# A query/key tile holds 32 channels of four heads in place of 64 channels of two, and one norm sum and root serve two tiles

## The chip, the cores and the metric

The kernel runs on one core of a Trainium2 chip. The metric is the time of one execution on the device in microseconds (us); the kernel is run several times and the median is shown. The core's engines have a queue of instructions each and run beside one another: TensorE (PE, matrix products, with a second queue PEld for loading weights), VectorE (DVE), ScalarE (ACT), GpSimd (POOL) and SyncE (SP, which here only starts transfers). An engine takes its instructions in order, so one that waits holds up everything behind it on that engine. Transfers run on 16 DMA engines.

## The reference

One layer of a hybrid encoder block on 1024 tokens of 1024 channels. After an RMS norm, one projection `z = h @ w_in` yields queries, keys and values for three attention groups of eight heads (64 channels each), and the gates and inputs of a gated linear recurrence. The part that the change concerns is the norm of queries and keys, for every token and every head over that head's 64 channels:

```
def rms_norm(t, w):
    t32 = t.astype(jnp.float32)
    return t32 * lax.rsqrt(jnp.mean(t32 * t32, axis=-1, keepdims=True) + EPS) * w.astype(jnp.float32)
...
for g, (window, dilation) in enumerate(ATTN_GROUPS):      # (128,1), (512,4), (2048,16)
    q = rms_norm(qkv_a[:, :, g, 0], q_norm_w[layer, g])
    k = rms_norm(qkv_a[:, :, g, 1], k_norm_w[layer, g])
    v = qkv_a[:, :, g, 2]
    o_g, m_g, d_g = dilated_window_attention(q, k, v, bias_tab[:, ...], window, dilation)
```

The attention takes scores `q . k` over the 64 channels of a head, adds a bias by distance, applies a softmax over a band of keys and sums the values. The recurrence branch, the two gates and the output projection follow and are left as they are.

## The kernel before

The program is straight-line code, written by a planner: class `Plan` keeps an estimated clock for each engine, and `Builder` emits instructions by it. Work that isn't on the main line stands in lists: `task` entries (for ACT, DVE, POOL and SP) and `product` entries (small matrix products for PE). `tick` emits a task when its inputs are due, by the plan's clocks, within `AHEAD` = 1.4 us of PE's clock; `burst` emits products between the main products. So the order on each engine is fixed when the program is built, from estimates, and the chip's waits follow from what really comes late. A `Ring` is a set of buffers of one kind, used in turn; a task can also wait for room in a ring.

The stages in order: normalising x and the value projections (to about 142 us); the **quads**, 27 blocks of the projection (142 to about 678 us); attention, mixed with projections of the recurrence's inputs (from about 685 us); the recurrence; the two output projections. The change lies in the quads and in what attention loads.

**A quad block** multiplies a 1024 x 512 piece of `w_in` with the whole input by a scheme with seven products in place of eight. Its weights come as four tiles `qraw` of 128 x 512 ("11", "12", "22", "21"), which SP loads into a ring of six (line 1098) in the order 11, 12, 22, 21 (`start_quads`, line 403). DVE subtracts tiles from one another (T1 = 12 - 11, T2 = 22 - 11 and so on); each operand is split into a high part `whi` (ACT copies it to the matmul's short float type) and a low part `wlo` (POOL, or DVE for T2 and T4, subtracts), into rings of `RING` = 9. Each of the seven products is 12 matmuls of 128 x 512 (`run_quads`, line 448). PE's order is 11(m), 22(m-1), T4(m-1), T1(m), T2(m), 21(m), T3(m), 11(m+1) and so on. Between the products ACT copies the accumulating bank `qA` after 11 and after T2, and `qE` after T1, and DVE adds the banks of 21, T3 and 22 to those copies: T2, T3 and T4 go on accumulating into `qA`, so a copy has to be out before the product after the next begins.

Twelve of the 27 blocks are query/key blocks (`qk`): group g (three), half hv of its heads (four heads each), e = 0 for queries and 1 for keys. They stand two at a time, with one or two other blocks after each two. A block's result is four tiles `z` of 128 channels x 512 tokens: col 0 or 1 (two heads of 64 channels each), half 0 or 1 of the tokens. In a `qk` block the weight tiles are read from rows of `w_in` in runs of 128 columns, so 512 bytes (`block_pages`, line 674).

**The norm** runs on each of the 48 tiles `z` by itself (lines 1124 to 1176): ACT squares z into a tile `ny` and copies it as `nhi`; DVE subtracts to get `nlo`; two matmuls with a matrix of ones, `headones` (ones in two diagonal blocks of 64 x 64), sum each head's 64 squares and spread the sum over the head's rows, in a PSUM bank `nss`; ACT takes Ln, Exp(-0.5 x) and a square; DVE ends with three operations (`newton`): a correction, z times weight (`nqk`) times root, and the two multiplied with the tokens put in the order of their residues. SP stores the tile to `qkD` in DRAM. Its rings: `ny` four, `nhi` and `nlo` two each, `spare` (z and other copies) seven.

**Attention** loads queries and keys of a (g, hv) whole, one transfer of 1 MB each, as tiles `aq` and `ak` of 128 x 2 x 1024 (`load_q` and `load_k`, lines 1253 to 1261): head 2a + i lies on the 64 partitions from 64 i, page a. Behind them come the bias `abias` and eight value tiles `av`. `scores` (line 1309) multiplies 64 partitions of `aq` and `ak` at a time into PSUM banks `sc`, and DVE adds the bias. For g = 0 one value tile is loaded as two transfers of 64 partitions (`load_v`, line 1263). The first such loads stand in SP's queue behind two transfers `stage<-h10D`.

## Time and profile before

| what | value |
|---|---|
| time, median of 3 runs (lowest, highest) | 1449.19 us (1448.72, 1449.32) |
| profiled execution: its own time, its span | 1449.3 us, 1447.5 us |
| PE busy | 1437.9 us, 99% of the span, 7930 matmuls |
| PEld busy | 1197.1 us |
| DVE, ACT, POOL busy | 967.6, 894.9, 338.8 us |
| DMA | 194992 packets, 230.75 MB; 46083 packets under 512 B |
| granted clock of PE | 1.0 |

The span runs from the first to the last instruction, and the execution's own time is 1.8 us longer. A busy share is the time in which an instruction of the engine was under way; the profile models a matmul's end, and matmuls overlap, so that the count of matmuls in a stretch says more than a matmul's own duration. "Idle before" is how long an engine waited ahead of the instruction, with the event that ended the wait. All matmul lines carry line 58, that of the recording wrapper, so rows are told apart by the tiles' names.

### The profile page before, as it was taken

The page shows a single profiled execution, that of the slowest core. Times are in us where ns is not written, and L with a number is a line of the kernel's source. Part 1 is how long each engine was busy: PE and PEld are TensorE (multiplying, and loading weights), DVE is VectorE, ACT ScalarE, POOL GpSimd, SP SyncE. Part 2 cuts the span into 40 slices and gives each one's busy share as a digit, 9 for nine tenths or more (in the row PEclk, how much of TensorE's full clock was granted, in tenths as well). Part 3 has the DMA queues.
Part 4 walks back from the last instruction along what each step waited for, and adds up shares of the span by engine and source line. Part 5 has one row for each costly group of instructions (what it writes and reads, how often), then busy time and mean ns, then how long its engine had stood idle before and what let it go on. Part 6 is the DMA issues. An engine that isn't in the chain of part 4 may idle for free.

```text
span 1447.5 us, 22946 instructions
## 1 busy us (share of the span) xinstructions
PE 1437.9 (99%) x7930; PEld 1197.1 (83%) x7930; DVE 967.6 (67%) x1901; ACT 894.9 (62%) x1900; POOL 338.8 (23%) x356
## 2 busy tenths in 40 slices
PE   9999999999999999999999999999999999999998
PEld 8788888888888888888788778888888888888887
DVE  6673677778685778331464648487878787358973
ACT  7743767566565676443688753397777774548461
POOL 0102334454423444333002000032222221001011
PEclk9999999999999999999999999999999999999999
DMA  7646567776643344324748439364444443678665
GB/s 239 181 141 197 167 195 164 196 152 167 151 124 102 102 103 115 111 103 142 267 147 292 156 101 331 120 148 103 130 106 129 107 136 87 215 243 213 189 167 137
DMA packets 194992, 230.75 MB, mean 159 GB/s; under 512 B 46083, under 2 KB 118043, under 8 KB 194364
## 3 DMA queue, kind: packets, MB, share of 16 engines
q1 hardware_dynamic: 180188, 203.93, 44.8%
q0 software_dynamic: 13824, 25.17, 11.3%
q8 instruction: 62, 1.02, 0.3%
q14 instruction: 54, 0.44, 0.1%
q10 hardware_dynamic: 864, 0.19, 0.1%
HBM read 169.29 MB, written 81.43 MB: 173 GB/s over the span
## 4 chain that ended last, share of the span: by engine, by line
PE 89%; DVE 6%; ACT 3%; issue 1%; DMA 1%; POOL 0%; SPq 0%; DVEq 0%
PE gp L58 27%; PE qA L58 20%; PE qE L58 10%; PE qC L58 5%; PE sA L58 5%; PE sE L58 4%; PE u L58 3%; PE oB L58 3%; PE o L58 3%; PE pT L58 2%; PE sc L58 2%; PE nss L58 2%; DVE Bc L58 1%; PE U L58 1%; DVE S L58 1%; DVE xs L58 1%
## 5 line engine op out<-in xcount | busy, mean ns | idle before, releaser
L58 POOL TENSOR_TENSOR wlo<-qraw,whi 128x512 fp32r<-128x512 f32 x135 | 191.7, 1425 | 380.9 <-ACT whi L58 294.4
L58 ACT ACTIVATE whi<-qraw 128x512 fp32r<-128x512 f32 x189 | 117.7, 626 | 100.6 <-DVE qraw L58 42.2
L58 DVE TENSOR_TENSOR qraw<-qraw,qraw 128x512 f32<-128x512 f32 x108 | 99.7, 924 | 36.7 <-POOL wlo L58 26.9
L58 PE MATMUL gp<-hh,whi 128*128 128x512 f32 x264 | 109.7, 416 | 0.0
L58 PE MATMUL gp<-hh,wlo 128*128 128x512 f32 x264 | 103.6, 393 | 0.0
L58 PE MATMUL gp<-hl,whi 128*128 128x512 f32 x264 | 103.0, 390 | 0.0
L58 ACT ACTIVATE as<-as,neg 128x192 f32<-128x192 f32 (+2 forms) x192 | 83.7, 440 | 18.0 <-DVE neg L58 17.9
L58 DVE CUSTOM_DVE_ANT_0 as<-sc,abias 128x192 f32<-128x192 f32 (+2 forms) x192 | 56.0, 348 | 43.7 <-PE sc L58 35.1
L58 ACT ACTIVATE whi<-raw 128x512 fp32r<-128x512 f32 x92 | 57.7, 627 | 43.9 <-PE gp L58 18.7
L58 PE MATMUL qA<-hh,whi 128*128 128x512 f32 x216 | 84.0, 389 | 0.0
L58 PE MATMUL qA<-hl,whi 128*128 128x512 f32 x216 | 84.0, 389 | 0.0
L58 PE MATMUL qA<-hh,wlo 128*128 128x512 f32 x216 | 84.0, 389 | 0.0
L58 POOL COPY mm<-Bc 128x8 f32<-128x8 f32 x64 | 32.2, 533 | 205.6 <-DVE Bc L58 123.6
L58 PE MATMUL gp<-whi,hh 128*128 128x512 f32 x192 | 78.6, 409 | 0.1
L58 PE MATMUL gp<-wlo,hh 128*128 128x512 f32 x192 | 75.2, 391 | 0.4 <-DVE wlo L58 0.4
L58 PE MATMUL gp<-whi,hl 128*128 128x512 f32 x192 | 75.0, 391 | 0.0
L58 DVE TENSOR_TENSOR wlo<-qraw,whi 128x512 fp32r<-128x512 f32 x54 | 37.3, 692 | 49.8 <-ACT whi L58 49.8
L58 DVE SCALAR_TENSOR_TENSOR ny<-ny,spare 128x512 f32<-128x512 f32 x48 | 63.2, 1316 | 1.6
L58 ACT ACTIVATE ny<-ny 128x512 f32<-128x512 f32 x96 | 60.8, 633 | 3.9 <-DVE ny L58 0.8
L58 PEld LDWEIGHTS gp<-hh,wlo 128*128 128x128 f32 x264 | 49.5, 188 | 11.0
L58 POOL DMA_DIRECT2D wlo<-in_w_in_dram x36 | 31.5, 875 | 113.6 <-ACT wlo L58 97.8
L58 ACT ACTIVATE stage<-gp 128x512 f32<-128x512 f32 x39 | 22.9, 591 | 54.9 <-PE gp L58 39.7
(306 smaller groups left out, 4232.2 us busy)
## 6 DMA issues: line engine op xcount, KB each, us to landing
qraw<-in_w_in_dram SPq DMA_DIRECT2D x108, 256.0 KB, 3.8
raw<-in_w_in_dram SPq DMA_DIRECT2D x84, 256.0 KB, 3.4
qkD<-ny SPq DMA_DIRECT2D x48, 256.0 KB, 2.8
wlo<-in_w_in_dram POOLq DMA_DIRECT2D x36, 256.0 KB, 4.1
sg<-sgD SPq DMA_DIRECT2D x32, 256.0 KB, 3.4
eraw<-wsD SPq DMA_DIRECT2D x32, 256.0 KB, 3.0
sgD<-stage SPq DMA_DIRECT2D x26, 256.0 KB, 2.6
ak<-qkD SPq DMA_DIRECT2D x6, 1024.0 KB, 6.2
```

The lines of the kernel that those rows point to most:

```text
L58: got = f(*args, **kw)
```

## The change

The channels of a `qk` block are dealt differently to its two columns: col 0 has channels 0 to 31 of all four heads, col 1 has channels 32 to 63. A row of `z` in col 0 and the same row in col 1 then belong to one head, so their squares can be added before the sum over rows, and the sum of a head (`headones` now has four blocks of 32 x 32) serves both tiles.

- The weights of a `qk` block are read in runs of 32 columns, 128 bytes, and each of the block's four tiles by four transfers, one for each head.
- `put_qk` waits until both columns of a half are there. Then ACT squares both, DVE adds the squares (`sq_sum`), ACT copies the high part (`sq_high`), DVE subtracts the low part, PE makes two matmuls, ACT takes Ln, Exp and square once; `newton` makes the correction once and the two products for each of the two columns, five operations of DVE in one go, and both are stored. A chain needs three tiles of the ring `ny` at its root, which still has four.
- The tile of norm weights has a column set for each col and is loaded by eight transfers in place of one.
- `aq` and `ak` are put together from four transfers each, of 32 partitions by 2 x 1024 (`load_heads`).

The order on each engine moves only in the quads; elsewhere on PE the rows are the same and in the same order. On PE 48 rows fall away, all of `nss`. Here PE's queue in the first `qk` blocks, names as above: before, two pairs of `nss` (of two tiles) between T2's last matmuls (`qA<-S1`) and the product 21 (`qC`),

```order
L58 MATMUL qA_1534<-S1h,wlo_1469 128x512
L58 MATMUL nss_1677<-nhi_1610,headones 128x512
L58 MATMUL nss_1677<-nlo_1641,headones 128x512
L58 MATMUL nss_1680<-nhi_1635,headones 128x512
L58 MATMUL nss_1680<-nlo_1653,headones 128x512
L58 MATMUL qC_1683<-hh_97,whi_1475 128x512
```

and of the changed kernel the only pair ahead of that product, one product earlier (`qE<-S0` is T1):

```order
L58 MATMUL qE_1639<-S0h,wlo_1476 128x512
L58 MATMUL nss_1670<-nhi_1629,headones 128x512
L58 MATMUL nss_1670<-nlo_1636,headones 128x512
L58 MATMUL qA_1562<-S1h,whi_1501 128x512
```

A pair now stands for two tiles, and there is one where there were two.

SP's queue in the quads, at the last two weight tiles of block 4, a `qk` block, and the first two of block 5, a gate (`qkD<-ny` stores a normed tile, `sgD<-stage` a gate's tile, `wsD` prepares later weights). Before:

```order
L58 DMA sgD<-stage_1836 128x512
L58 DMA wsD<-in_w_proj_b_dram 16x4096
L58 DMA qkD<-ny_1882 128x512
L58 DMA qraw_1959<-in_w_in_dram 128x4x128
L58 DMA qraw_1961<-in_w_in_dram 128x4x128
L58 DMA qraw_1967<-in_w_in_dram 128x512
L58 DMA qraw_1969<-in_w_in_dram 128x512
L58 DMA sgD<-stage_1856 128x512
```

and now:

```order
L58 DMA skewD<-tabD 128x384
L58 DMA wsD<-in_w_proj_b_dram 16x4096
L58 DMA qraw_1961<-in_w_in_dram 128x4x32 x4
L58 DMA qraw_1970<-in_w_in_dram 128x4x32 x4
L58 DMA qraw_1975<-in_w_in_dram 128x512
L58 DMA qraw_1977<-in_w_in_dram 128x512
L58 DMA sgD<-stage_1882 128x512
```

Each `qk` weight tile is four issues where it was one, and the loads that follow and the stores behind them stand as many issues later; no `qkD` store stands ahead of them here any more.

SP's queue at the start of attention, before:

```order
L58 DMA stage_6205<-h10D 128x512
L58 DMA ak_6207<-qkD 128x2x1024
L58 DMA aq_6209<-qkD 128x2x1024
L58 DMA abias_6211<-skewD 128x4x256
L58 DMA av_6213<-vD 128x256
```

and now:

```order
L58 DMA stage_6094<-h10D 128x512
L58 DMA ak_6096<-qkD 32x2x1024 x4
L58 DMA aq_6101<-qkD 32x2x1024 x4
L58 DMA abias_6106<-skewD 128x4x256
L58 DMA av_6108<-vD 128x256
```

The order is the same, with four issues in place of one for keys and for queries, and each covers a quarter of the partitions.

The diff, without the renaming of the constant `half_ones` to `part_ones`:

```diff
@@ -407,6 +407,10 @@
             src = self.quads[m][("11", "21", "12", "22").index(b)]
+            if isinstance(src, list):
+                for i, x in enumerate(src):
+                    self.p.sp.dma_start(raw[m, b].rearrange("p (d a c) -> p a d c", d=4, a=4)[:, i], x)
+                return
@@ -683,7 +687,8 @@
         p = 24 * g + 8 + 8 * hv
-        return tuple(_dram(wi, (p + 4 * k) * 65536 + 128 * (2 * e + col), [[512, 128], [65536, 4], [1, 128]])
+        return tuple([_dram(wi, (p + 4 * k) * 65536 + 256 * e + 32 * col + 64 * i, [[512, 128], [65536, 4], [1, 32]])
+                      for i in range(4)]
@@ -818,7 +823,7 @@
-    nqk = consts.tile([128, 6], F32, name="nqk")
+    nqk = consts.tile([128, 2, 6], F32, name="nqk")
@@ -830,8 +835,8 @@
     def bias_tables(p):
-        g_.tensor_scalar(nqk[:, 0:3], nqk[:, 0:3], -0.125 / 128.0, None, op0=OP.mult)
-        g_.tensor_scalar(nqk[:, 3:6], nqk[:, 3:6], -1.0 / 128.0, None, op0=OP.mult)
+        g_.tensor_scalar(nqk[:, :, 0:3], nqk[:, :, 0:3], -0.125 / 128.0, None, op0=OP.mult)
+        g_.tensor_scalar(nqk[:, :, 3:6], nqk[:, :, 3:6], -1.0 / 128.0, None, op0=OP.mult)
@@ -988,7 +993,9 @@
         if d == 3:
-            s_.dma_start(nqk, a["qk_w"])
+            for c in range(2):
+                for k in range(4):
+                    s_.dma_start(nqk[32 * k:32 * k + 32, c], a["qk_w"][32 * c:32 * c + 32])
@@ -1102,8 +1109,8 @@
         a_.preload_act_table_set("natural_log_exp_and_others")
-        v_.tensor_copy(blk["ones"].rearrange("p (j c) -> p j c", j=2),
-                       half_ones[:, :, None].to_broadcast([128, 2, 64]))
+        v_.tensor_copy(blk["ones"].rearrange("p (j c) -> p j c", j=4),
+                       part_ones[:, :, None].to_broadcast([128, 4, 32]))
@@ -1122,58 +1129,76 @@
     def put_qk(g, hv, e):
+        have = {}
+
...
                 a_.activation(z, ps, AF.Copy)
-            b.task("act", [z], lambda: squares(g, hv, e, half, col, z), 3, lambda: blk["y"].soon() and blk["hi"].soon())
+            zs = have.setdefault(half, {})
+            zs[col] = z
+            if len(zs) == 2:
+                b.task("act", list(zs.values()), lambda: squares(g, hv, e, half, zs), 3, lambda: blk["y"].soon(2))
...
-    def squares(g, hv, e, half, col, z):
-        sq, hi = blk["y"].get(), blk["hi"].get()
-        a_.activation(sq, z, AF.Square)
+    def squares(g, hv, e, half, zs):
+        sq, other = blk["y"].get(), blk["y"].get()
+        a_.activation(sq, zs[0], AF.Square)
+        a_.activation(other, zs[1], AF.Square)
+        b.task("dve", [sq, other], lambda: sq_sum(g, hv, e, half, zs, sq, other), 3)
+
+    def sq_sum(g, hv, e, half, zs, sq, other):
+        v_.tensor_tensor(sq, sq, other, op=OP.add)
+        blk["y"].done(other)
+        b.task("act", [sq], lambda: sq_high(g, hv, e, half, zs, sq), 3, blk["hi"].soon)
+
+    def sq_high(g, hv, e, half, zs, sq):
+        hi = blk["hi"].get()
         a_.activation(hi, sq, AF.Copy)
-        b.task("dve", [hi], lambda: sq_low(g, hv, e, half, col, z, sq, hi), 3, blk["lo"].soon)
-
-    def sq_low(g, hv, e, half, col, z, sq, hi):
+        b.task("dve", [hi], lambda: sq_low(g, hv, e, half, zs, sq, hi), 3, blk["lo"].soon)
+
+    def sq_low(g, hv, e, half, zs, sq, hi):
...
         blk["y"].done(sq)
-        b.product(0, [lo], lambda: head_sums(g, hv, e, half, col, z, hi, lo), b.gps.soon, merge=False, banks=0)
-
-    def head_sums(g, hv, e, half, col, z, hi, lo):
+        b.product(0, [lo], lambda: head_sums(g, hv, e, half, zs, hi, lo), b.gps.soon, merge=False, banks=0)
+
+    def head_sums(g, hv, e, half, zs, hi, lo):
...
         blk["lo"].done(lo)
-        b.task("act", [ps], lambda: guess(g, hv, e, half, col, z, ps), 3, lambda: blk["y"].soon(2))
-
-    def guess(g, hv, e, half, col, z, ps):
-        y, y2 = blk["y"].get(), blk["y"].get()
+        b.task("act", [ps], lambda: guess(g, hv, e, half, zs, ps), 3, lambda: blk["y"].soon(3))
+
+    def guess(g, hv, e, half, zs, ps):
+        y, y2, z1 = (blk["y"].get() for _ in range(3))
...
         a_.activation(y2, y, AF.Square)
-        b.task("dve", [y2], lambda: newton(g, hv, e, half, col, z, ps, y, y2), 3)
-
-    def newton(g, hv, e, half, col, z, ps, y, y2):
+        b.task("dve", [y2], lambda: newton(g, hv, e, half, zs, ps, y, y2, z1), 3)
+
+    def newton(g, hv, e, half, zs, ps, y, y2, z1):
...
         k = g + 3 * e
-        v_.scalar_tensor_tensor(z, z, nqk[:, k:k + 1], y, op0=OP.mult, op1=OP.mult)
         R = (1, 4, 8)[g]
+        n = 512 // R
         res = lambda t: t.rearrange("p (u r) -> p r u", r=R) if R > 1 else t
-        v_.scalar_tensor_tensor(y.rearrange("p (r u) -> p r u", r=R) if R > 1 else y, res(y2), -192.0, res(z),
-                                op0=OP.add, op1=OP.mult)
+        per = lambda t: t.rearrange("p (r u) -> p r u", r=R) if R > 1 else t
+        for col in (0, 1):
+            z = zs[col]
+            v_.scalar_tensor_tensor(z, z, nqk[:, col, k:k + 1], y, op0=OP.mult, op1=OP.mult)
+            o = y if col else z1
+            v_.scalar_tensor_tensor(per(o), res(y2), -192.0, res(z), op0=OP.add, op1=OP.mult)
+            blk["spare"].done(z)
+
+            def out(o=o, col=col):
+                s_.dma_start(qkD[g, hv, 2 * e + col].rearrange("p (r u) -> p r u", r=R)[:, :, n * half:n * half + n],
+                             o.rearrange("p (r u) -> p r u", r=R))
+                blk["y"].done(o)
+            b.task("sp", [o], out, 1)
         blk["y"].done(y2)
-        blk["spare"].done(z)
-
-        def out():
-            n = 512 // R
-            dst = qkD[g, hv, 2 * e + col].rearrange("p (r u) -> p r u", r=R)[:, :, n * half:n * half + n]
-            s_.dma_start(dst, y.rearrange("p (r u) -> p r u", r=R))
-            blk["y"].done(y)
-        b.task("sp", [y], out, 1)
@@ -1250,14 +1275,20 @@
+    def load_heads(t, g, hv, k):
+        for j in range(2):
+            for c in range(2):
+                s_.dma_start(t[64 * j + 32 * c:64 * j + 32 * c + 32],
+                             qkD[g, hv, k + c].rearrange("(a i d) t -> i d a t", a=2, i=2)[j])
+
...
         KT[g, hv] = att["k"].get()
-        s_.dma_start(KT[g, hv], qkD[g, hv, 2:4].rearrange("a p t -> p a t"))
+        load_heads(KT[g, hv], g, hv, 2)
...
         QT[g, hv] = att["q"].get()
-        s_.dma_start(QT[g, hv], qkD[g, hv, 0:2].rearrange("a p t -> p a t"))
+        load_heads(QT[g, hv], g, hv, 0)
```

10 lines of the change are left out of this document (5 added, 5 removed).

## The prediction

> **What bounds the kernel now.** I read the page's first part, then the chain of waits, then the table of stretches.
>
> ```profile
> PE 1437.9 (99%) x7930; PEld 1197.1 (83%) x7930; DVE 967.6 (67%) x1901; ACT 894.9 (62%) x1900; POOL 338.8 (23%) x356
> PE 89%; DVE 6%; ACT 3%; issue 1%; DMA 1%; POOL 0%; SPq 0%; DVEq 0%
> PE gp L58 27%; PE qA L58 20%; PE qE L58 10%; PE qC L58 5%; PE sA L58 5%; PE sE L58 4%; PE u L58 3%; PE oB L58 3%; PE o L58 3%; PE pT L58 2%; PE sc L58 2%; PE nss L58 2%; DVE Bc L58 1%; PE U L58 1%; DVE S L58 1%; DVE xs L58 1%
> ```
>
> PE is the bound, and `nss`, the norm sums, stands in the chain by name. A busy share alone could hide slow matmuls, so the stretches (length, PE busy and its matmuls, PEld, DVE, ACT, POOL, granted clock, DMA share, GB/s):
>
> ```profile
> 122.00:560.00 438.00, 438.00 (x1934) 362.69 (x1933) 313.53 (x374) 277.39 (x475) 181.04 (x142) 1.00 0.57 146
> 560.00:655.00 95.00, 95.00 (x420) 78.67 (x420) 45.63 (x58) 45.95 (x78) 33.25 (x26) 1.00 0.39 120
> ```
>
> In the first row lie nearly all norms, in the second none: 438.00/1934 and 95.00/420 are 0.226 us for a matmul in both. So while the norms run, PE takes one matmul after another without a hole, at full clock, and a matmul taken out is worth its whole slot.
>
> **PE's saving.** The tile view of `nss` gives the number, the timeline the slot:
>
> ```profile
> L58 PE MATMUL nss<-nhi,headones x48: 389/389/389, 158.9 to 561.0; 128*128 128x512 f32 x48
> ```
>
> ```profile
> 199.44 0.39 PE L58 MATMUL qA<-hh,wlo 128*128 128x512 f32 x1
> 199.66 0.39 PE L58 MATMUL nss<-nhi,headones 128*128 128x512 f32 x1
> 199.89 0.39 PE L58 MATMUL nss<-nlo,headones 128*128 128x512 f32 x1
> ```
>
> The three start 0.22 and 0.23 us apart: `nss` takes a slot like any other matmul, 0.2265 us by the first stretch. 96 of them become 48: 48 x 0.2265 = 10.9 us less.
>
> **ACT and DVE.** Groups of the norm (count, busy us, mean ns, idle before):
>
> ```profile
> L58 DVE SCALAR_TENSOR_TENSOR ny<-ny,spare 128x512 f32<-128x512 f32 x48 | 63.2, 1316 | 1.6
> L58 ACT ACTIVATE ny<-ny 128x512 f32<-128x512 f32 x96 | 60.8, 633 | 3.9 <-DVE ny L58 0.8 <-DMA qkD<-ny 0.2
> L58 DVE SCALAR_TENSOR_TENSOR spare<-spare,nqk,ny 128x512 f32<-128x512 f32 x48 | 49.4, 1029 | 0.0
> L58 DVE TENSOR_TENSOR nlo<-ny,nhi 128x512 fp32r<-128x512 f32 x48 | 45.4, 947 | 9.2 <-ACT nhi L58 9.1
> L58 DVE SCALAR_TENSOR_TENSOR ny<-nss,ny 128x512 f32<-128x512 f32 x48 | 32.9, 686 | 7.5 <-ACT ny L58 7.4
> L58 ACT ACTIVATE ny<-nss,eps 128x512 f32<-128x512 f32 x48 | 32.5, 676 | 1.1 <-DMA qkD<-ny 0.9
> L58 ACT ACTIVATE nhi<-ny 128x512 fp32r<-128x512 f32 x48 | 30.4, 633 | 1.5
> ```
>
> Each of the 24 chains saves ACT one copy, one Ln and two of `ny<-ny`, 2.58 us, 62 us in all; DVE saves 0.95 + 0.69 and adds one sum, priced as the subtraction (0.95): 0.7 us, 16 us. Both engines have holes in this stretch (313.5 and 277.4 us busy of 438), so I count none of it. On the other side a root's last task is now five DVE operations in a row, 0.69 + 2 x (1.03 + 1.32) = 5.4 us where it was 3.0; what queues behind it are DVE's additions of PE's banks. The tightest, T3's, has two products (5.4 us) until T4 writes the bank and takes 0.7 itself: 2.4 us of delay fits. I take 0.
>
> **The weight tiles in pieces of 128 bytes.** A tile of 512-byte pieces now (four issues; then the loads' times from issue to landing, and a stretch in which little but these tiles moves):
>
> ```profile
> 201.51 2.02 SPq L58 DMA_DIRECT2D qraw<-in_w_in_dram  x4
> ```
>
> ```profile
> DMA to landing us min/median/max: 2.4/3.8/7.5
> ```
>
> ```profile
> 124.00:128.00 4.00, 4.00 (x19) 3.34 (x18) 0.69 (x1) 1.23 (x2) 1.29 (x1) 1.00 1.10 302
> ```
>
> An issue is about 0.5 us, and 256 KB at 302 GB/s are 0.87 us. The 48 tiles of the `qk` blocks become 192 transfers with four times the pieces. A tile's last issue comes 3 x 0.5 = 1.5 us later. The transfer costs between 0.87 us (bytes decide) and four times that (pieces decide), so up to 2.6 us more. The nearest rows for smaller pieces are the stores of normed tiles, first 512-byte runs (group 1, 310 to 435 us), then 256-byte runs (group 2, 450 to 580 us), the tile view of `qkD` by stretches:
>
> ```profile
> DMA to landing us min/median/max: 2.6/2.6/3.4
> ```
>
> ```profile
> DMA to landing us min/median/max: 2.8/2.9/4.4
> ```
>
> Twice the pieces cost 0.3 us, so I take 0.3 + 0.6 = 0.9 us for four times, and a tile 2.4 us later at its last byte. Even at the upper end the mean DMA share rises from 0.57 by 48 x 2.6/438 = 0.28, to 0.85.
>
> Who waits? The product that uses a tile comes late: the first `whi<-qraw` and the first `qA` matmul, and the last of each, by their tile views:
>
> ```profile
> L58 ACT ACTIVATE whi<-qraw x189: 614/624/637, 125.2 to 653.9; 128x512 fp32r<-128x512 f32 x189
> L58 PE MATMUL qA<-hh,whi x216: 389/389/389, 142.5 to 677.7; 128*128 128x512 f32 x108
> ```
>
> The first product starts 17 us after its split, the last 22 to 24, so operands aren't late. But DVE and ACT are in order. DVE's T2 takes tile "22" (the first of the four issued at 201.51) almost as it lands:
>
> ```profile
> 204.85 0.69 DVE L58 TENSOR_TENSOR qraw<-qraw,qraw 128x512 f32<-128x512 f32 x1 [1.12 <-POOL wlo L58]
> 207.64 0.62 ACT L58 ACTIVATE whi<-qraw 128x512 fp32r<-128x512 f32 x1
> 212.60 0.58 ACT L58 ACTIVATE spare<-qA 128x512 f32<-128x512 f32 x1
> 214.17 0.39 PE L58 MATMUL qA<-S2h,whi 128*128 128x512 f32 x1
> ```
>
> Behind the split of T2 on ACT stands the copy of `qA`, which has to be out before T3's `S2` matmul writes that bank. The room: T2's result is ready at 205.54 and waits 2.1 us, and the copy ends at 213.18, 1.0 us before T3; ACT's smaller holes between I leave out. So "22" may come 3.1 us later than now; it will be 2.4. I take 0, with a loss from 3.1 us on. The stores behind a burst of loads stand up to 12 issues (6 us) later; `ny` or `stage` tiles come free as much later, which is in the third rival.
>
> The Trainium skill, DMA: Bandwidth & Descriptors, Specifications, sets 512 bytes as the least for full rate and says that shorter writes are read, modified and written. The two store rows show no such jump at 256 bytes; no row here shows 128-byte loads.
>
> **The start.** Seven more issues for `nqk` fall into a hole of SP between 23.2 and 29.67 us:
>
> ```profile
> 22.76 0.42 SPq L58 DMA_DIRECT2D oh<-in_c_onehot_dram  x1
> 29.67 21.51 SPq L58 DMA_DIRECT2D raw<-in_w_in_dram  x8
> ```
>
> At 0.42 us each they are 2.9 us: nothing.
>
> **Queries and keys in quarters.** Here PE does wait for a transfer. The first scores, and the loads:
>
> ```profile
> 696.34 2.22 PE L58 MATMUL sc<-ak,aq 64*128 64x192 f32 x24 [1.48 <-issue]
> ...
> 686.16 0.37 SPq L58 DMA_DIRECT2D ak<-qkD  x1
> 686.58 0.46 SPq L58 DMA_DIRECT2D aq<-qkD  x1
> ```
>
> ```profile
> 686.50:695.00 8.50, 8.37 (x37) 6.58 (x36) 1.38 (x2) 3.15 (x4) 0.00 (x0) 1.00 0.98 344
> ```
>
> The hole of 1.48 us is labelled "issue", but `sc` needs only `ak` and `aq`, and the 2.1 MB issued at 686 to 687 take 6.1 us at 344 GB/s, behind two `stage` tiles of 256 KB (1.5 us) and with the 1.5 us that a lone tile needs beyond its transfer (2.4 - 0.87): they land at about 696. So each microsecond that they land later is one of PE. Nothing else is left for PE there. Six more issues cost 2.5 us of SP, under the transfer. The rate is open: no row has a load into 32 partitions. The nearest are the value loads of g = 0, in SP's order 64 KB into the lower 64 partitions, 64 KB into the upper 64, 128 KB into all (start, then landing, tile view of `av` at three times):
>
> ```profile
> L58 SPq DMA_DIRECT2D av<-vD x1: 617/617/617, 774.0 to 774.0; - x1
> DMA to landing us min/median/max: 4.4/4.4/4.4
> ...
> L58 SPq DMA_DIRECT2D av<-vD x1: 481/481/481, 774.7 to 774.7; - x1
> DMA to landing us min/median/max: 4.1/4.1/4.1
> ...
> L58 SPq DMA_DIRECT2D av<-vD x1: 429/429/429, 775.2 to 775.2; - x1
> DMA to landing us min/median/max: 3.9/3.9/3.9
> ```
>
> They land at 778.4, 778.8 and 779.1: 0.4 us for the second half tile, 0.3 us for the whole tile of twice the bytes. So a part of the partitions takes at least twice as long per byte. Bounds: 0 and 6.1 us (twice the time). Pieces for the lower and upper half follow one another on the same engines and can overlap a little, so I take 4.0. The later five pairs are loaded many microseconds ahead of their scores; 0.
>
> The Trainium skill, SBUF — State Buffer, Door 1: The DMA port swizzle, says that 32 or 64 adjacent partitions reach 8 of 16 ports: 189 GB/s at 1 MiB in place of 328. By that an estimate is 11.1 us for 6.4, 4.7 more, and a time of 1443.0. The `av` rows agree.
>
> **Sum.** 1449.3 - 10.9 + 4.0 = 1442.4, against the profiled execution, which is 0.1 above the median: **1442.3 us**.
>
> **Rivals.** First, the quarters load as fast as the whole: 1449.2 - 10.9 = 1438.3. For it: the same engines carry the same bytes; against it: the `av` rows. Second, the slow side: pieces decide, "22" lands over 3.1 us late, and ACT's copy of `qA` holds T3 in each `qk` block. At the upper end, 1.5 + 2.6 = 4.1 us late, that is 1 us in each of 12 blocks: 1442.3 + 12 = 1454.3. For it: DMA shares above the mean in places, where landings already reach 7.5 us; against it: the small price of 256-byte pieces. Third, partial stalls from the chain: `ny` has four tiles and a root needs three, so a second chain's Ln waits on ACT for the first one's stores, late behind 16 issues; 0.3 us of PE for each of 24 chains is 7 us, and with the 4.0 the result is 1449.5, no change. For it: the queue of SP; against it: ACT now has 62 us more room. That the sums aren't halved is excluded by the rows of PE's queue.
>
> **Numbers.** Forecast 0.55 (1440 to 1445.5), first rival 0.25, second 0.07, third 0.13. The range 1437.8 to 1447.0 holds the first two and a part of the third, 0.82. A measurement of this kernel can tell about 0.2% (2.9 us) from no change: faster 0.86 (the first two and a third of the third), same 0.07, slower 0.07.
>
> **What will show it.** Right: 48 `nss` matmuls in all, PE without holes to 680 us, the first `sc` idle by about 5 us. Wrong: PE idle ahead of `qA<-S2` or `qE`, released by ACT (second or third rival); `sc` waiting about 1.5 us as now (first); `qraw` landings far above 6 us.

## The result: 1.2% slower, and the profile after

| | median (lowest, highest), us | ratio to before, 95% interval |
|---|---|---|
| before | 1449.19 (1447.35, 1449.48) | |
| changed | 1465.91 (1463.87, 1468.51) | 1.0123 (1.0112 to 1.0134) |

The prediction was 1442.3 us, 7 us faster; the changed kernel is 17 us slower. The execution that was profiled took 1468.5 us, 2.6 above the median, so the losses read from its profile are that much larger than those between the medians. The head of its page, then the tile views of `nss`, of one form of the `qA` matmuls and of `sc` (count, shortest/median/longest ns, first and last start):

```profile
PE 1438.4 (98%) x7882; PEld 1191.7 (81%) x7882; DVE 946.5 (65%) x1879; ACT 834.7 (57%) x1804; POOL 333.6 (23%) x356
PE 58%; DVE 7%; ACT 5%; DMA 3%; issue 2%; SPq 1%; POOL 0%; DVEq 0%; ACTq 0%
```

```profile
L58 PE MATMUL nss<-nhi,headones x24: 388/389/398, 168.6 to 573.0; 128*128 128x512 f32 x24
L58 PE MATMUL qA<-hh,whi x216: 389/389/500, 142.8 to 685.3; 128*128 128x512 f32 x108
L58 PE MATMUL sc<-ak,aq x384: 272/323/524, 704.3 to 861.6; 64*128 64x192 f32 x80, 64*128 64x128 f32 x64, 64*128 64x256 f32 x48
```

The norm sums are halved: 24 of each kind, 7882 matmuls for 7930. But PE's share of the chain of waits fell from 89% to 58%, a sign that PE now waits for others. Where, is read from the first and last starts. The quads run from 142.8 to 685.3, 542.5 us; before it was 142.5 to 677.7 (shown in the prediction), 535.2. They got 7.3 us longer where the sum had them 10.9 shorter: 18 us lost. The scores run from 704.3 to 861.6, 157.3 us; before:

```profile
L58 PE MATMUL sc<-ak,aq x384: 272/323/481, 696.3 to 843.1; 64*128 64x192 f32 x80, 64*128 64x128 f32 x64, 64*128 64x256 f32 x48
```

146.8 us, so another 10.5 us were lost there. The stretches say the same (columns as in the prediction):

```profile
122.00:560.00 438.00, 426.95 (x1862) 349.01 (x1861) 287.59 (x345) 213.62 (x373) 172.63 (x140) 1.00 0.65 146
560.00:655.00 95.00, 93.77 (x413) 76.97 (x412) 48.12 (x59) 45.99 (x78) 32.69 (x26) 1.00 0.38 117
690.00:820.00 130.00, 122.61 (x1048) 101.25 (x1047) 61.81 (x341) 89.58 (x332) 14.03 (x21) 0.96 0.81 214
```

PE has 11 us of holes in the first where it had none, and in 690 to 820 us 7.4 us and a lower granted clock; before, the same stretch had 2.0 us of holes at clock 1.00. The groups of PE's matmuls in the quads (142 to 690 us) that had idle time before them name who ended it:

```profile
L58 PE MATMUL qA<-hh,whi 128*128 128x512 f32 x216 | 84.7, 392 | 6.0 <-DVE stage L58 4.2 <-DVE spare L58 1.8
L58 PE MATMUL qA<-S2h,whi 128*128 128x512 f32 x108 | 42.8, 396 | 3.4 <-ACT stage L58 2.3 <-ACT spare L58 1.0
...
L58 PE MATMUL nss<-nlo,headones 128*128 128x512 f32 x24 | 9.7, 403 | 2.9 <-DVE nlo L58 2.9
```

Three waits: product T4 (`qA<-hh`; the row also counts product 11, but all the holes are T4's) for DVE, product T3 (`qA<-S2`) for ACT, the norm sum for its operand from DVE.

**T4.** The timeline around the longest of its holes (start, duration, the idle time before in brackets):

```profile
361.94 0.39 PE L58 MATMUL qA<-S2h,wlo 128*128 128x512 f32 x1
369.60 0.50 PE L58 MATMUL qA<-hh,whi 128*128 128x512 f32 x1 [1.83 <-DVE stage L58]
...
362.33 0.69 DVE L58 SCALAR_TENSOR_TENSOR ny<-nss,ny 128x512 f32<-128x512 f32 x1 [1.99 <-ACT ny L58]
362.94 1.79 DVE L58 SCALAR_TENSOR_TENSOR spare<-spare,nqk,ny 128x512 f32<-128x512 f32 x1
364.77 2.42 DVE L58 SCALAR_TENSOR_TENSOR ny<-ny,spare 128x512 f32<-128x512 f32 x1
367.11 0.74 DVE L58 SCALAR_TENSOR_TENSOR spare<-spare,nqk,ny 128x512 f32<-128x512 f32 x1
367.88 1.06 DVE L58 SCALAR_TENSOR_TENSOR ny<-ny,spare 128x512 f32<-128x512 f32 x1
368.86 0.69 DVE L58 TENSOR_TENSOR stage<-qA,stage 128x512 f32<-128x512 f32 x1
...
362.90 1.29 POOL L58 TENSOR_TENSOR wlo<-qraw,whi 128x512 fp32r<-128x512 f32 x1 [1.13 <-ACT whi L58]
...
364.70 1.56 POOL L58 TENSOR_TENSOR wlo<-qraw,whi 128x512 fp32r<-128x512 f32 x1
```

T3's last matmul ends at 362.33, and at the same moment DVE begins the five operations of a root. They take 6.5 us (two of them stand beside a subtraction of POOL's and take 1.8 and 2.4 us instead of 0.7 to 1.1), and T3's addition starts 6.53 us late. Until T4 there are two products, 24 x 0.2265 = 5.4 us, less the addition's own 0.7: room for 4.7. The hole is 6.53 - 4.7 = 1.83. Worked out in the same way from the timeline, the other five late additions (5.78, 5.92, 5.08, 5.41 and 5.48 us) give holes of 1.07, 1.22, 0.38, 0.70 and 0.79 us: each is its lateness less 4.7. In the kernel before, the latest of the 27 additions is 2.34 us late.

**The norm sum.** The longest hole of the quads:

```profile
231.66 0.39 PE L58 MATMUL nss<-nhi,headones 128*128 128x512 f32 x1
234.79 0.50 PE L58 MATMUL nss<-nlo,headones 128*128 128x512 f32 x1 [2.75 <-DVE nlo L58]
...
236.69 0.63 PE L58 MATMUL qC<-hh,whi 128*128 128x512 f32 x1
237.12 0.63 PE L58 MATMUL qC<-hl,whi 128*128 128x512 f32 x1
...
231.28 1.78 DVE L58 TENSOR_TENSOR ny<-ny,ny 128x512 f32<-128x512 f32 x1
232.98 2.35 DVE L58 TENSOR_TENSOR nlo<-ny,nhi 128x512 fp32r<-128x512 f32 x2
```

PE's order has the norm sum at 231.7, but DVE begins the added sum of squares of the second chain only at 231.3 and the low parts at 233.0. The first chain's high part had been ready on ACT at 229.5; its low part stands on DVE behind that sum of squares of the second chain. Behind the hole the matmuls stand 0.43 us apart in place of 0.23 for some 3 us, and the granted clock from 234.8 to 239.0 us is 0.65: 9 x 0.2 = 1.8 us more, so this hole costs over half as much again.

**Attention.** The first scores, then the timeline near 800 us, where the longest hole of the program is:

```profile
704.31 0.56 PE L58 MATMUL sc<-ak,aq 64*128 64x192 f32 x2 [1.80 <-issue]
706.43 0.94 PE L58 MATMUL sc<-ak,aq 64*128 64x192 f32 x7 [1.56 <-DMA aq<-qkD]
...
787.64 6.72 SPq L58 DMA_DIRECT2D av<-vD  x8
794.46 0.97 SPq L58 DMA_DIRECT2D raw<-in_w_in_dram  x2
795.48 1.87 SPq L58 DMA_DIRECT2D aq<-qkD  x4
...
797.84 0.63 ACT L58 ACTIVATE whi<-raw 128x512 fp32r<-128x512 f32 x1 [0.22 <-DMA raw<-in_w_in_dram]
800.69 0.63 ACT L58 ACTIVATE whi<-raw 128x512 fp32r<-128x512 f32 x1 [2.22 <-DMA raw<-in_w_in_dram]
...
803.24 1.06 ACT L58 ACTIVATE stage<-gp 128x512 f32<-128x512 f32 x2
...
803.87 0.79 PE L58 MATMUL gp<-whi,hh 128*128 128x512 f32 x1 [3.38 <-ACT stage L58]
```

```profile
698.00:706.00 8.00, 5.07 (x22) 3.68 (x21) 0.04 (x1) 1.89 (x2) 0.00 (x0) 1.00 1.04 214
```

At the first scores the quarters cost 1.4 us (1.80 + 1.56 for 1.48 and a second hole of 0.44). While they move, the engines are fully busy (share 1.04) at 214 GB/s; whole tiles had 344 at 0.98 (shown in the prediction). The larger part is paid later: for the following pairs, tiles `raw` of unrelated weights stand behind the quarters, ACT waits for them, the copies of PE's banks (`stage<-gp`) stand behind on ACT, and PE waits 3.4 us. Behind this hole the granted clock is 0.50 from 803.8 to 809 us, half of the full clock: by estimate another 2.6 us.

### The profile page after: what moved, and what is told of

It reads as the page before. It is cut to its first block, busy times and chain, and to the rows that moved or that the text cites. A ratio compares the mean times of both kernels' runs of the same rounds, so it can differ in the third digit from the quotient of the medians.

```text
span 1466.4 us, 23042 instructions
## 1 busy us (share of the span) xinstructions
PE 1438.4 (98%) x7882; PEld 1191.7 (81%) x7882; DVE 946.5 (65%) x1879; ACT 834.7 (57%) x1804; POOL 333.6 (23%) x356
## 3 DMA queue, kind: packets, MB, share of 16 engines
q8 instruction: 62, 1.02, 0.3%
## 4 chain that ended last, share of the span: by engine, by line
PE 58%; DVE 7%; ACT 5%; DMA 3%; issue 2%; SPq 1%; POOL 0%; DVEq 0%; ACTq 0%
PE gp L58 21%; PE qA L58 10%; PE qE L58 5%; PE sA L58 4%; PE sE L58 4%; PE o L58 3%; PE oB L58 3%; PE pT L58 2%; PE qC L58 2%; PE sc L58 2%; DVE ny L58 1%; DVE Bc L58 1%; DVE spare L58 1%; PE U L58 1%; DVE S L58 1%
## 5 line engine op out<-in xcount | busy, mean ns | idle before, releaser
L58 POOL TENSOR_TENSOR wlo<-qraw,whi 128x512 fp32r<-128x512 f32 x135 | 187.1, 1393 | 393.6 <-ACT whi L58 364.4
L58 DVE TENSOR_TENSOR qraw<-qraw,qraw 128x512 f32<-128x512 f32 x108 | 87.9, 814 | 45.5 <-DMA qraw<-in_w_in_dram 29.3
L58 DVE SCALAR_TENSOR_TENSOR ny<-ny,spare 128x512 f32<-128x512 f32 x48 | 67.2, 1400 | 1.6
L58 ACT ACTIVATE spare<-qA 128x512 f32<-128x512 f32 x51 | 30.3, 593 | 55.5 <-PE qA L58 52.6
L58 PEld LDWEIGHTS gp<-hh,whi 128*128 128x128 f32 x264 | 49.8, 189 | 8.4
```

The lines of the kernel that those rows point to most:

```text
L58: got = f(*args, **kw)
```

## The experiments

Times are medians; the kernel before was run beside each. The last column is the idle time ahead of three groups of PE's matmuls between 142 and 690 us (to 790 us in `heads` and `both`, whose quads are longer), as in the group view above.

| kernel | us | ratio to before (95%) | PE's waits in the quads ahead of T4, T3, `nss`, us |
|---|---|---|---|
| before | 1449.2 | | 0, 0, 0 |
| changed | 1465.9 | 1.0112 to 1.0134 | 6.0, 3.4, 2.9 |
| `raw512` | 1461.8 | 1.0069 to 1.0108 | 4.8, 1.3, 2.9 |
| `before_pieces` | 1456.4 | 1.0032 to 1.0062 | 0, 4.4, 0.9 |
| `before_four_issues` | 1449.7 | 0.9990 to 1.0009 | 0, 0, 0 |
| `before_quarters` | 1459.0 | 1.0060 to 1.0094 | 0, 0, 0 |
| `heads` | 1547.0 | 1.0652 to 1.0711 | 4.7, 69.4, 12.1 |
| `both` | 1524.1 | 1.0490 to 1.0536 | 3.6, 45.8, 11.5 |
| `whole` | 1452.1 | 1.0014 to 1.0038 | 4.8, 1.5, 2.6 |
| `whole_split` | 1457.7 | 1.0049 to 1.0085 | 0, 0.9, 10.1 |
| `whole_split_late` | 1459.0 | 1.0061 to 1.0091 | 0.7, 0.8, 9.1 |
| `whole_late5` | 1455.8 | 1.0030 to 1.0066 | 4.5, 2.3, 5.5 |
| `whole_four` | 1457.4 | 1.0048 to 1.0080 | 7.0, 1.2, 4.0 |
| `whole_four_late5` | 1439.1 | 0.9919 to 0.9951 | 0, 0, 0 |
| `whole_four_late4` | 1440.2 | 0.9921 to 0.9954 | 1.9, 0, 0 |
| `whole_four_late7` | 1441.1 | 0.9923 to 0.9956 | 0, 1.0, 0 |
| `whole_hold` | 1453.3 | 1.0016 to 1.0042 | 0, 0.5, 7.9 |
| `whole_hold_late5` | 1453.2 | 1.0020 to 1.0046 | 0, 1.9, 7.9 |
| `whole_hold_late5_store5` | 1460.3 | 1.0058 to 1.0092 | 0, 1.5, 10.7 |
| `after_four_late5` | 1453.5 | 1.0024 to 1.0045 | 1.0, 1.9, 0 |

### The pieces of the weight tiles

`raw512` takes the pieces out of the change; the second part orders the columns of a page of `w_in` on the host:

```diff
-        return tuple([_dram(wi, (p + 4 * k) * 65536 + 256 * e + 32 * col + 64 * i, [[512, 128], [65536, 4], [1, 32]])
-                      for i in range(4)]
+        return tuple(_dram(wi, (p + 4 * k) * 65536 + 128 * (2 * e + col), [[512, 128], [65536, 4], [1, 128]])
...
+    four = np.arange(512).reshape(2, 4, 2, 32).transpose(0, 2, 1, 3).reshape(-1)
```

> The change as it is, but the host orders the 256 query (and key) columns of a page so that a tile's 128 channels are adjacent again: each qraw tile is one transfer of 512-byte runs, as before the change. The quads of the changed kernel lost 18 us against the sum (7.4 longer instead of 10.9 shorter). Theory L (the late pieces of the weight tiles hold DVE and ACT, and these PE): the 18 us come back, 1465.9 - 18 = 1448, PE without holes over 0.3 us between 142 and 683 us. Theory C (the longer chain with its extra hop and five DVE operations in a row holds them): within 2 us of 1465.9, the holes ahead of qA<-hh and nss<-nlo stay.

1461.8: 4 us came back, not 18. Theory C (the chain) has most of it.

`before_pieces` puts them into the kernel before:

```diff
-        return tuple(_dram(wi, (p + 4 * k) * 65536 + 128 * (2 * e + col), [[512, 128], [65536, 4], [1, 128]])
+        return tuple([_dram(wi, (p + 4 * k) * 65536 + 128 * (2 * e + col) + 32 * i, [[512, 128], [65536, 4], [1, 32]])
+                      for i in range(4)]
```

> The kernel before, each qk weight tile loaded by four transfers of 32 columns (128-byte runs) instead of one of 512-byte runs; the same bytes into the same places. Theory L: the loads alone cost what the quads lost, 1449.2 + 18 = 1467. Theory C: within 2 us of 1449.2. Both together: between, about 1455 to 1460.

1456.4: 6.8 us, between the theories. Issues or small pieces? `before_four_issues` has the same four transfers for a tile, each of one 128-column piece of 512 bytes, with every instruction in the same place as in `before_pieces` (the diff is against the kernel before):

```diff
-        return tuple(_dram(wi, (p + 4 * k) * 65536 + 128 * (2 * e + col), [[512, 128], [65536, 4], [1, 128]])
+        return tuple([_dram(wi, (p + 4 * k + i) * 65536 + 128 * (2 * e + col), [[512, 128], [1, 128]])
+                      for i in range(4)]
```

> The kernel before, each qk weight tile in four transfers of 128 columns of one page each, so with 512-byte pieces; every instruction stands where it does in the run with 128-byte pieces (1456.4). If the four issues are the cost: 1456 again. If the 128-byte pieces are: 1449.

1449.7: no cost. The timelines of the first `qk` blocks, with 128-byte pieces and then with 512-byte ones:

```profile
144.32 7.91 SPq L58 DMA_DIRECT2D qraw<-in_w_in_dram  x10
...
151.17 0.69 DVE L58 TENSOR_TENSOR qraw<-qraw,qraw 128x512 f32<-128x512 f32 x1 [6.51 <-DMA qraw<-in_w_in_dram]
...
153.92 0.63 ACT L58 ACTIVATE whi<-qraw 128x512 fp32r<-128x512 f32 x1 [1.39 <-DMA qraw<-in_w_in_dram]
154.45 0.58 ACT L58 ACTIVATE spare<-qA 128x512 f32<-128x512 f32 x1
...
155.09 0.50 PE L58 MATMUL qA<-S2h,whi 128*128 128x512 f32 x1 [2.08 <-ACT spare L58]
```

```profile
143.74 4.85 SPq L58 DMA_DIRECT2D qraw<-in_w_in_dram  x10
...
148.13 0.69 DVE L58 TENSOR_TENSOR qraw<-qraw,qraw 128x512 f32<-128x512 f32 x1 [3.55 <-DMA qraw<-in_w_in_dram]
```

With small pieces even the ten issues take 3.1 us longer and the tile is used 3.0 us later; ACT's copy of `qA` stands behind a split that waits for its own late tile, and T3 starts after a hole of 2.1 us. That is the way of the prediction's second rival, though not at the split of T2 that it named. The next two holes of T3, 1.02 and 0.86 us, came another way. Around the first of them, with the 128-byte pieces:

```profile
434.44 0.53 SPq L58 DMA_DIRECT2D qkD<-ny  x1
437.16 0.63 ACT L58 ACTIVATE ny<-ny 128x512 f32<-128x512 f32 x1 [3.63 <-DMA qkD<-ny]
438.69 0.59 ACT L58 ACTIVATE stage<-qA 128x512 f32<-128x512 f32 x1
439.33 0.50 PE L58 MATMUL qA<-S2h,whi 128*128 128x512 f32 x1 [1.02 <-ACT stage L58]
```

The store of a `ny` tile stands behind 16 issues of weight tiles (424.6 to 434.4 us), ACT waits 3.63 us for it, and the copy of `qA` stands behind. With 512-byte pieces the same wait is 2.38 us and T3 is in time. In all the quads ACT waits for such stores 8.6 us with the small pieces, 3.1 with 512-byte ones, 1.1 in the kernel before and 0.9 in the changed kernel. That is the way of the third rival. So it is the size of the pieces that costs, and both rivals' ways show, in the kernel before.

### Whole tiles of queries and keys

`heads` stores the normed rows so that `ak` and `aq` can be read whole, `both` joins that with `raw512`:

```diff
-                s_.dma_start(qkD[g, hv, 2 * e + col].rearrange("p (r u) -> p r u", r=R)[:, :, n * half:n * half + n],
+                s_.dma_start(qkD[g, hv, 2 * e:2 * e + 2].rearrange("a (i c d) (r u) -> (a i) c d r u", i=2, c=2, r=R)
+                             [:, col, :, :, n * half:n * half + n],
```

> The change, but the stores of the normed tiles put their rows where the whole ak and aq tile can be read in one transfer of 128 partitions, as before the change; the weight tiles still come in four pieces. Theory A (the quarters cost the 10.5 us that the stretch from the last product of the quads to the last scores got longer): 1465.9 - 10.5 = 1455.4, the first sc idle about 1.5 us, no hole of 3 us near 800. Rival (the attention stretch suffers from what comes before it: clock and later loads): over 1461.

> Host order and row order together: adjacent channels in the loads, whole ak and aq tiles; only the shared norm sums are left of the change. L and A both right: 1465.9 - 18 - 10.5 = 1437.4, which is the sum of the prediction without its 4.0 (1438.3). C right: about 1455. If the two losses aren't independent: between.

Both missed by far: 1547.0 and 1524.1 us. The scores took 147 us again, but the quads got 97 and 72 us longer than in the change and in `raw512`. In the stretch of `heads` below hardly anything but two such stores moves (columns as above):

```profile
350.80:352.80 2.00, 2.00 (x11) 1.65 (x10) 1.24 (x3) 0.90 (x2) 2.00 (x2) 1.00 0.28 79
```

A share of 0.28 and 79 GB/s. The address of such a store has an outer dimension of 4, where the other stores have the 128 rows. The Trainium skill, DMA: Bandwidth & Descriptors, Why a DMA increments its semaphore by 16 and not by 1, says that the number of DMA engines for a transfer is the largest, up to 16, that divides the outer dimension of both sides; that would be 4 here, and a quarter of the engines busy fits the row. The number of engines itself isn't in the trace.

`whole` avoids this: the host deals the columns so that a tile's row is (head pair, channel, head), the stores stay as in the change, and the load is one transfer again:

```diff
-        for j in range(2):
-            for c in range(2):
-                s_.dma_start(t[64 * j + 32 * c:64 * j + 32 * c + 32],
-                             qkD[g, hv, k + c].rearrange("(a i d) t -> i d a t", a=2, i=2)[j])
+        s_.dma_start(t.rearrange("p a t -> p (a t)"), qkD[g, hv, k:k + 2].rearrange("c (x a) t -> x c (a t)", a=2))
...
+    four = np.arange(512).reshape(2, 2, 2, 2, 32).transpose(0, 3, 2, 4, 1).reshape(-1)
```

> The shared norm sums with everything around them as before the change: the host orders the columns so that a tile's row is (head pair, channel, head), the weight tiles come in one transfer of 512-byte runs, the stores are as in the change, and ak and aq are each read in one transfer of 128 partitions. Theory A (the quarters cost the 10.5 us of the attention): 1461.8 (adjacent columns alone) - 10.5 = 1451, no hole near 800 us, the first sc idle 1.5 us. Rival (the attention lost them through the order of work that follows the quads): over 1458.

`before_quarters` does the opposite:

```diff
-        s_.dma_start(KT[g, hv], qkD[g, hv, 2:4].rearrange("a p t -> p a t"))
+        for q in range(0, 128, 32):
+            s_.dma_start(KT[g, hv][q:q + 32], qkD[g, hv, 2:4, q:q + 32].rearrange("a p t -> p a t"))
```

(and the same for `QT`).

> The kernel before, ak and aq each read by four transfers of 32 partitions instead of one of 128; nothing else. Theory A: 1449.2 + 10.5 = 1459.7, with a hole of some us near 795. The prediction's step: 1449.2 + 4.0 = 1453.2, all of it ahead of the first sc. Rival of the prediction: 1449.2.

1452.1 and 1459.0: 9.7 us less without the quarters, 11 us more with them. Theory A holds in both directions, and the kernel before with quarters has the same hole at the same place:

```profile
795.84 0.61 PE L58 MATMUL gp<-whi,hh 128*128 128x512 f32 x1 [3.94 <-ACT stage L58]
```

What is left is the shared norm sum by itself: 1452.1, where the sum of PE's work says 1438.3. Nearly 14 us are lost in the chain alone.

### The chain

All that follows starts from `whole`. First, the root's scalings as tasks of their own (`whole_split`; "the last" in its expectation is `whole`), then also the norm sum later in PE's order (`whole_split_late`; there "the last" is `whole_split`):

```diff
+        def scaled(col):
+            v_.scalar_tensor_tensor(z, z, nqk[:, col, k:k + 1], y, op0=OP.mult, op1=OP.mult)
+            b.task("dve", [z], lambda: rooted(col), 3)
...
+        b.task("dve", [y2], lambda: scaled(0), 3)
```

```diff
-            if max(self.when(t) + self.SLACK, self.bank.when(t.banks)) > self.p.t["pe"]:
+            if max(self.when(t) + (self.SLACK if t.banks else 2.5), self.bank.when(t.banks)) > self.p.t["pe"]:
```

> As the last, and the Newton step's four scalings are tasks of their own on DVE, so that other work can stand between them. Theory R (the run of five DVE operations, stretched by POOL's subtractions to 6 to 8 us, makes the addition of T3's bank late and so T4): the holes ahead of qA<-hh (4.8 us in all with adjacent columns) go, 1451 - 5 = 1446. Rival (DVE is late for other reasons): no change against the last.

> As the last, and the norm sum's two matmuls are put into PE's order only 2.5 us after the planned end of their operand instead of 0.6 us. If the hole of 2.7 us ahead of nss<-nlo with the dip of the clock behind it (158 matmuls for 178 in the 40 us, 20 x 0.2265 = 4.5 us) comes from DVE being later than planned: 4 to 5 us less than the last, about 1442. If PE's order wasn't the cause: no change.

The waits of T4 went as expected (4.8 to 0 us), but those of `nss` grew from 2.6 to 10.1, and to 9.1 with the margin of 2.5: slower in all. Theory R was right about T4 and wrong about the time.

Next, the five operations kept together and the margin 5 (`whole_late5`, 5.0 for 2.5 in the diff above); the root in four operations (`whole_four`: the root times its correction once, then one scaling for each col, of which the diff shows the two new lines); and both:

```diff
         v_.scalar_tensor_tensor(y2, ps, 64.0 * EPS, y2, op0=OP.add, op1=OP.mult)
+        v_.scalar_tensor_tensor(y, y2, -192.0, y, op0=OP.add, op1=OP.mult)
...
+            v_.scalar_tensor_tensor(per(o), res(zs[col]), nqk[:, col, k:k + 1], res(y), op0=OP.mult, op1=OP.mult)
```

> The shared norm sums with whole tiles (1452.1), and the norm sum's two matmuls put into PE's order only 5 us after the planned end of their operand instead of 0.6 us; Newton's five operations in one run as in the change. Theory H (the chain crosses ACT and DVE once more, runs behind its plan, and PE meets nss before its operand is there): the hole of 2.46 us and the dip of the clock behind it (160 for 178 matmuls, 4 us) go, the holes ahead of qA<-hh (4.9 us) stay: about 1448. Rival (a later norm only moves the wait to the tiles that come free later): 1452 or more.

> The shared norm sums with whole tiles, and Newton's factor worked out once for both columns: (y2 - 192) y first, then one scaling for each column, four DVE operations in a row in place of five, about 1.0 to 1.3 us less. Theory R (the run of DVE holds T3's addition): the holes ahead of qA<-hh (1.36, 1.65, 0.37, 0.67, 0.80) become smaller by 1.0 to 1.3 us each, so about 3.5 us less in all: 1448.5. If the run isn't what holds it: 1452.

> Both of these together: four operations, nss 5 us later. H and R: 1452.1 - 4 - 3.5 = 1444.5, below the kernel before. If the whole saving of PE came through it would be 1438.

Each alone made it slower (1455.8, 1457.4), against H and against R. In `whole_four` the shorter run also began later: around 315 us ACT's square for the root waits 2.41 us until DVE is done with a `ny` tile, the run starts at 315.7, and T3's addition is 6.3 us late, hardly less than with five operations. Together the two edits gave 1439.1, faster than the kernel before by 0.65%; since each alone was a loss, that isn't the sum of H and R. Its stretch and its `qA` matmuls:

```profile
122.00:560.00 438.00, 438.00 (x1930) 361.25 (x1929) 276.71 (x338) 225.94 (x392) 175.19 (x144) 1.00 0.58 151
```

```profile
L58 PE MATMUL qA<-hh,whi x216: 389/389/389, 142.0 to 667.4; 128*128 128x512 f32 x108
```

PE has no hole left, and the quads take 525.4 us, 9.8 less than before: the saving that the prediction counted.

Is that one lucky order? With margins of 4 and 7 us:

> As the fastest, with nss 4 us later in place of 5. The waits for nss' operand seen so far are 2.4 to 2.8 us long at a margin of 0.6, so 4 us should do: 1439 to 1442. If the order of one margin only is lucky: 1450 or more.

> As the fastest (four operations, nss 5 us later: 1439.1), but nss 7 us later. If the later norm sum is a robust remedy: 1439 again, within 2 us. If 5 us met a lucky place for the roots: holes ahead of qA<-hh come back, 1450 or more.

1440.2 and 1441.1, no wait ahead of `nss` in either. The remedy holds at the three margins tried, 4, 5 and 7 us. At 4 one wait of T4 is left, 1.86 us: a subtraction on DVE beside POOL took 5.71 us, and with the root behind it T3's addition came 7.02 us late. And on the change as given:

> The change as given, pieces of 128 bytes and quarters included, with the root in four operations and nss 5 us later in PE's order. If the three losses are independent: 1439.1 + 10 (quarters: 1459.0 - 1448.0 = 11, 1461.8 - 1452.1 = 9.7) + 4 to 7 (pieces: 1465.9 - 1461.8, 1456.4 - 1449.6) = 1453 to 1456. If the late pieces bring the root back ahead of T3's addition: over 1460.

1453.5, the lower end of what was expected: 14.4 above the same chain with whole tiles. The losses of quarters (about 10) and pieces (about 4) add up.

What do the two edits do? `whole_hold` keeps five operations but forbids a root on DVE while the products 21 and T3 are issued; then the margin; then stores handed to SP later:

```diff
-        b.task("dve", [y2], lambda: newton(g, hv, e, half, zs, ps, y, y2, z1), 3)
+        b.task("dve", [y2], lambda: newton(g, hv, e, half, zs, ps, y, y2, z1), 3, lambda: b.now not in ("21", "T3"))
...
-            b.task("sp", [o], out, 1)
+            b.task("sp", [o], out, 1, after=b.p.done(o) + 5.0)
```

> The shared norm sums with whole tiles, five operations and nss as in the change; but no root is handed to DVE while the products 21 and T3 are being issued, so that none stands ahead of T3's addition. Theory R (the place of the root): no T3 addition more than 4.7 us after its bank, the holes ahead of qA<-hh (4.9 us, with their slower restarts 5.5) go: 1452.1 - 5.5 = 1446.6, the holes ahead of nss stay. Rival (chain as a whole too long): 1452 or more.

> The shared norm sums with whole tiles, Newton's five operations in one run as in the change, no root handed to DVE during the products 21 and T3, and nss 5 us later. If the two waits (T4 for T3's addition, PE for nss' operand) are all that eats the saving, and the length of the run by itself costs nothing: 1439 to 1442, no hole over 0.3 us in the quads. If the four operations of the fastest kernel were what made it work: 1450 or more.

> As the last kernel with the root held and nss 5 us later (1453.2), and each store of a normed tile is handed to SP only 5 us after the planned end of its tile, so that the loads of weight tiles aren't queued behind a store that waits. If the loop (late root, store waits on SP, next weight tiles late, DVE waits, next norm late) is what is left: the holes ahead of nss (7.9 us) go, with their restarts 10 us: 1443. If nss is late for other reasons: 1450 or more.

`whole_hold`: the T4 waits are gone, as theory R says, but `nss` waits 7.9 us in place of 2.6, and the time stays (1453.3). `whole_hold_late5`: the same (1453.2), so a margin of 5 us doesn't help a chain with five operations. One such place:

```profile
219.19 1.71 SPq L58 DMA_DIRECT2D qkD<-ny  x2
221.00 3.15 SPq L58 DMA_DIRECT2D qraw<-in_w_in_dram  x4
...
226.92 0.69 DVE L58 TENSOR_TENSOR qraw<-qraw,qraw 128x512 f32<-128x512 f32 x1 [3.97 <-DMA qraw<-in_w_in_dram]
...
232.00 0.50 PE L58 MATMUL nss<-nlo,headones 128*128 128x512 f32 x1 [3.41 <-DVE nlo L58]
```

On SP the stores wait for the root, the next weight tiles behind them, DVE for those tiles, and the next norm behind DVE. At the same place ACT's squares of the second chain also wait 1.53 us (225.6) for such a store to free a `ny` tile, so the ring of four has a part. Taking the stores out of the way (`whole_hold_late5_store5`) cut DVE's waits for weight tiles in the quads from 20.9 to 4.0 us, but the time rose to 1460.3, since `nss` now waits for ACT:

```profile
534.78 2.17 ACT L58 ACTIVATE ny<-spare 128x512 f32<-128x512 f32 x4
...
537.52 0.79 PE L58 MATMUL nss<-nhi,headones 128*128 128x512 f32 x1 [4.27 <-ACT nhi L58]
```

So taking out that loop alone doesn't bring the norm sums in time. The edit also keeps each `ny` tile 5 us longer, so whether the loop has a part in their being late stays open.

Shown is that the waits ahead of T4 come from the root's place in DVE's order: in `whole_split` and `whole_hold` they go from 4.8 to 0 us. Shown is also that the time follows the three waits together: the runs built on `whole` with 8.4 to 12.3 us of them take 1452.1 to 1460.3 us, those with 0 to 1.9 us take 1439.1 to 1441.1. An edit that removed the waits at one place let them grow at another. Open is why `nss` is in time at margins of 4, 5 and 7 us with four operations and late at 5 with five: the shorter run, its tiles free earlier, or merely where the planner puts the rest.

## Why the prediction was wrong, step by step

- **PE's saving (10.9 us).** Right, as an amount of work: 48 matmuls fewer, and 9.8 us in `whole_four_late5`, where nothing waits. The premise that PE takes matmul after matmul held only for the kernel before.
- **ACT and DVE ("so I count none of it"; "2.4 us of delay fits. I take 0").** This is the step that failed, by 13.8 of the 23.6 us by which the forecast was missed. It compared the growth of the root (5.4 for 3.0 us) with the room of T3's addition. What the addition can have ahead of it is the whole run. 5.4 us by its own price is already more than 4.7, and the trace shows 6.5. The growth alone would have left nothing either: the latest addition before was already 2.34 us late, and with 2.4 more the room of 4.7 is used up. And it only asked about the run of DVE operations; the added hop (sum on DVE, high part on ACT, low part on DVE, then PE) wasn't costed, and the waits ahead of `nss` come on top. "Both engines have holes" was true (65% and 57% busy in the changed kernel) and no argument: the waits are at two places in order.
- **Weight tiles in pieces ("I take 0, with a loss from 3.1 us on").** The loss named here did come, 4.1 us in the change and 6.8 in the kernel before. The size was off: tiles came about 3.0 us later where 2.4 were taken. The price from the 256-byte stores was too low for 128-byte loads; the issues, which had 1.5 of the 2.4 us, are free with 512-byte pieces. The Trainium skill, DMA: Bandwidth & Descriptors, Specifications, sets 512 bytes as the least for full rate, which the prediction held against the 256-byte stores; these 128-byte loads agree so far that they were slower than 512-byte ones. At which size between them the rate falls, and whether by reading and modifying, no run shows. The second rival's 12 us, with a wait in every block, was too much: `before_pieces` has three waits of T3 over 0.2 us, and only the largest came the way that this rival described.
- **The start: 0.** Right; the first product starts at 142.8 after 142.5.
- **Quarters (+4.0 at the first scores, 0 for the later five pairs).** Right in direction, wrong in place. At the first scores 1.4 us, since the scores of one head need only half of the partitions and begin when these are there. The later pairs are indeed early enough, but they occupy the transfers at little over half the rate, and the unrelated tiles behind them are late: about 10 us in all. The estimate by the Trainium skill, SBUF — State Buffer, Door 1: The DMA port swizzle (4.7 us) was for the transfer too, not for what stands behind it; its lower rate for 32 adjacent partitions agrees with the rows (214 GB/s for 344).
- **The sum.** 1449.2 - 10.9 = 1438.3; with the chain 1452.1, with quarters 1461.8, with pieces 1465.9. The miss of 23.6 us is 13.8 of the chain, 5.7 of the quarters (9.7 for 4.0) and 4.1 of the pieces.
- **Rivals.** The first (quarters free) is refuted. The third, partial stalls from the chain, was given 0.13 and a time of 1449.5. Stalls from the chain did come and cost twice its 7 us, but not by its mechanism: in the changed kernel ACT waited for `ny` stores to land only 0.9 us in all the quads. The place was DVE's order. No rival had the time that came, and the 0.07 for "slower" had no working of its own but the second rival's. The chance of "faster", the first two and a third of the third, is 0.55 + 0.25 + 0.04 = 0.84 and not 0.86.
- **"What will show it".** "PE without holes to 680 us" failed in the way named as wrong (waits ahead of `qA<-S2`), and in two ways not named, T4 and `nss`. The 48 `nss` matmuls came as said; the first `sc` were idle for 1.80 and 1.56 us and not for about 5.

## What to carry to other kernels

Where engines take their work in order, idle time doesn't make an added operation free: look at the tightest consumer (here an addition with 4.7 us of room) and put the whole run that can stand ahead of it against that room, not the difference to the run that stood there. Longer chains that cross engines need a margin at the point where the bound engine meets them. An edit that removes one such wait can let another grow: here a margin gained time only together with the shorter root. And a slower transfer is paid by what stands behind it in the queue, even when its own user isn't waiting.

## What the runs showed of the hardware that was not expected

- Stores of the same tiles with their rows dealt to an outer dimension of 4 ran at 79 GB/s with the DMA engines 28% busy, and cost 72 us (`both` at 1524.1, `whole` at 1452.1 us).
- PE can be slow behind a hole. In the quads every hole of 2.38 us or more was followed by matmuls 0.43 us apart in place of 0.23 (after 2.75 us for some 3 us, at a granted clock of 0.65), and no single hole up to 1.65 us was. Between, the length alone doesn't decide: after 1.83 us (changed kernel, 369.6 us) and 2.08 us (`before_pieces`, 155.1) the rate was full again, while after 1.84 us (`whole_four`, 488.1) and 2.08 us (`both`, 312.4) it fell from the seventh matmul on. The Trainium skill, TensorE: Matmul & The Clock Gate, Part 1, tells of a halved clock after an idle window of about 3.4 us; here shorter holes were enough.
- 128-byte pieces made some of SP's own issues longer: ten in 7.91 us, with 512-byte pieces in 4.85. The median of one hardly differs (0.48 and 0.43 us); a few take up to 1.75 us.
- DVE operations on two tiles of SBUF took 1.8 to 2.4 us instead of 0.7 to 1.1 beside one of POOL's subtractions. Beside several of them in a row it was up to 4.86 us (`whole_four_late5`, 330.4) and 5.71 us (`whole_four_late4`, 330.5).
